# Modulation of layer 0 in a two-layer transformer kernel: weights as the stationary operand

## The chip, the cores and the metric

The kernel runs on one core of one Trainium2 chip. The metric is the device time of one execution in microseconds, taken as the median of a few runs. A profile of one execution goes with it. TensorE appears in the profile as two rows: PE for the streaming of the moving operand, PEld for the loading of the stationary operand.

## The reference, cut to what matters

Two transformer layers work on 1024 latent tokens and 256 context tokens of width 1024. Each layer starts from a modulation: a vector `silu(c)` for the latent tokens, and a second one, `silu(c_ctx)`, for the context tokens, are multiplied by the layer's `ada_w` (1024 x 6144). The first two sixths of the product are the shift and the scale of the first norm.

```
silu_c = jax.nn.silu(c);  silu_cc = jax.nn.silu(c_ctx)
mod_l = silu_c @ ada_w[i] + ada_b[i]      # and mod_c with silu_cc
sh1, sc1, g1, sh2, sc2, g2 = jnp.split(mod, 6)
a = rms_norm(h, norm_mix[i]) * (1.0 + sc1) + sh1
q, k, v = split(a @ w_qkv)                # then attention, output, FFN
```

The change concerns only shift and scale (`sh1`, `sc1`) of layer 0, which are needed before any projection of that layer can start: 1024 x 2048 weights, two input vectors.

## The kernel before, in words

Tensors lie by feature: 128 features on the partitions, eight blocks of features (`kc` or `m`, 0 to 7), tokens on the free axis. The tokens come in three blocks: 0 and 1 are the latent tokens (512 each), 2 is the context (256).

Everything of interest happens in `startup()`, the first 115 us. Its order is not left to a scheduler: each step is a generator, started at a planned time, and a heap of planned times decides in which order the instructions are written into the queues of the engines (TensorE, VectorE, ScalarE, GpSimd, and SyncE for all transfers). A planned time is thus only a rank. On the chip each engine takes its queue strictly in order and waits where an input is missing. The steps:

- `loads()` queues all transfers on SyncE: the eight modulation tiles `aw` (1 MB each, three buffers), the tokens `x` of block 0 between the first of them, raw weights of the first K, Q and V products, the tokens of blocks 1 and 2 (block 2 takes an `aw` buffer), two copies of the broadcast vectors to memory (`Cd`, for later modulations), more raw weights, and 40 small transfers for the position bias.
- `c_rows()` (L348 to L352) broadcasts the two silu vectors over all partitions: a diagonal on VectorE, a product with a matrix of ones on TensorE (four of 512 columns), a copy on ScalarE into `crow`.
- `stat(b)` (L363 to L382) gives the root mean square of a block: eight squares on ScalarE, six additions on VectorE and GpSimd, two products with ones on TensorE (L373), logarithm and exponential on ScalarE. Block 0 is then multiplied by the result on VectorE (L382).
- `modulation(m)` (L397 to L409), once for each block of features. The shift: two multiply-and-reduce passes of VectorE over the transposed weights and `crow` (L400), one for each vector. The scale: eight products on TensorE with the two vectors as the stationary operand and 128 columns of weights moving (L397), which gives two rows; ScalarE copies them out (L403), TensorE turns them into columns (L407). Three small VectorE instructions add the biases and form the gain (L404, L408, L409).
- `apply0(kc)` (L419 to L423) makes the normalised block 0 as a high part on ScalarE and a low part on GpSimd; `apply(b, kc)` (L431, L432, and `norm_lo` at L131 to L134) does the same for blocks 1 and 2, with VectorE in it.
- `first_qk(b)` (lines L770 to L772 in `dense_steps`) multiplies a block with the first K and Q weights, three products for each block of features because high and low parts are multiplied separately; `vals0` (L786 to L788 in `proj_v`) makes the V tiles, 128 tokens at a time. `first_qk(0)` takes block kc only after the modulation of block kc + 3 is written.

The queue order on TensorE from L373 on is, before: modulation 3 and 4, two kc of `first_qk(0)`, modulation 5, 6 and 7 with single kc between them, the other kc of block 0, four V tiles, block 1, two V tiles, block 2, four V tiles.

Of the kernel before, what the change touches and what calls it, by code (L numbers as in the profile page):

```python
# [10 lines left out]
F32 = mybir.dt.float32  # L11
F32R = mybir.dt.float32r
ALU = mybir.AluOpType
# [5 lines left out]
P = 128  # L19
D = 1024  # L20
KC = D // P
# [10 lines left out]

V_NMIX, V_NFFN, V_NFIN, V_B, V_QG, V_KG, V_C = 0, 16, 32, 40, 136, 137, 138
V_N = 154
CFG = dict(lag=3, tv=8.0, tm=5.0, t1=43.0, t2=58.0, p0=28, lo="GD", n=39, ra=2.3, rc=0.7, rq=1.1, rb=1.05, gap=263, r1=1.262, lh=300, tk='ADAG', tb=1000000000.0, tg=1, lp='GD')
PERIOD1 = 8172
ORDER1 = {
# [35 lines left out]
def _build(tc, nc, I, O, top):  # L73
    v, s, g, t = nc.vector, nc.scalar, nc.gpsimd, nc.tensor
# [17 lines left out]
    ident = const.tile([P, P], F32, name="ident")  # L92
# [6 lines left out]
    def vec(base, k):  # L99
        return vecs[:, base + k:base + k + 1]  # L100
# [166 lines left out]
    def startup():  # L267

        ET = mybir.EngineType
        with ExitStack() as ph:  # L270
# [29 lines left out]
            def loads():  # L300
                W = I["wqkv0"]
                for m in range(KC):
                    load_aw(m)
                    yield 2.9
                    if m < 2:
                        load_x(0, m)
                        yield 2.9
                    if m in (2, 4):
                        k = "k" if m == 2 else "q"
                        load_raw(k, W[8 if m == 2 else 0])  # L310
                        start(now + 3.5, split(k, wsp))
                        yield 1.5
                for i in range(2):
                    load_raw(f"v{i}", W[16:18, :, i * 512:i * 512 + 512])
                    start(now + CFG["tv"], split(f"v{i}", w0))
                    yield 1.5
                for i in range(2):
                    load_x(1, i)
                    yield 2.9
                xs.append(tmp.tile([P, KC, 256], F32, name="aw", bufs=3))  # L320
                load_x(2, 0, 1)
                yield 2.9
                for w in range(2):
                    dma(out=Cd[w], in_=crow[w][:])
                    yield 1.5
                for m in (1, 9):
                    load_raw(f"u{m}", W[m])
                    yield 1.5
                for _ in bias_steps():
                    yield 0.7  # L330
# [12 lines left out]
            def c_rows():  # L343
                for w in range(2):
                    for i in range(2):
                        ps = psm.tile([P, 512], F32, name="ps1")
                        dg = tmp.tile([P, 4, P], F32, name="nsq", bufs=2)
                        v.tensor_tensor(dg[:], ident[:].unsqueeze(1).broadcast_to([P, 4, P]),  # L348
                                        silc2[:, 4 * i:4 * i + 4, w:w + 1].broadcast_to([P, 4, P]), ALU.mult)
                        t.matmul(ps[:], lhsT=ones[:], rhs=dg[:].rearrange("p a n -> p (a n)"), start=True, stop=True)  # L350
                        yield 0.8
                        s.mul(crow[w][:, i * 512:i * 512 + 512], ps[:], float(D))  # L352
                        yield 0.3

            def stat(b):
                n = BLK[b][1]
                acc = []
                for kc in range(KC):
                    if b == 0 and kc == 4:
                        yield 3.6  # L360
                    sq = tmp.tile([P, n], F32, name="nsq", bufs=2) if kc > 1 else \
                        tmp.tile([P, n], F32, name=("nacc", "nacb")[kc], bufs=1)
                    s.activation(sq[:], xs[b][:, kc, :], AF.Square)  # L363
                    if kc > 1:
                        i = kc in (3, 6)
                        (v, g)[i].tensor_tensor(acc[i][:], acc[i][:], sq[:], ALU.add)
                    else:
                        acc.append(sq)
                    yield 0.55
                yield CFG["tm"] if b == 1 else 2.0  # L370
                ms = psp.tile([P, 512], F32, name="ms")
                for i in range(2):
                    t.matmul(ms[:, :n], lhsT=ones[:], rhs=acc[i][:], start=i == 0, stop=i == 1)  # L373
                yield 2.0
                rs[b] = tmp.tile([P, n], F32, name="nrs", bufs=1)
                s.activation(rs[b][:], ms[:, :n], AF.Ln, bias=eps[:])
                s.activation(rs[b][:], rs[b][:], AF.Exp, scale=-0.5)
                acts[b] = new_act(b)
                yield 0.9
                if b == 0:  # L380
                    for kc in range(KC):
                        v.tensor_tensor(xs[0][:, kc, :], xs[0][:, kc, :], rs[0][:], ALU.mult)  # L382
                        start(now + 0.9, apply0(kc))
                        yield 0.7
                    return
                for kc in range(KC):
                    start(now, apply(b, kc))
                    yield 1.1 if b == 1 else 0.7

            raw0 = tmp.tile([P, KC, 2], F32, name="raw0", bufs=1)  # L390
            ready = set()

            def modulation(m):

                rows = psp.tile([2, P], F32, name="rw", bufs=2)
                for kc in range(KC):
                    t.matmul(rows[:], lhsT=silc2[:, kc, :], rhs=aws[m][:, 1, kc * P:kc * P + P], start=kc == 0, stop=kc == KC - 1)  # L397
                for w in range(2):
                    junk = tmp.tile([P, D], F32, name="adaj", bufs=1)
                    v.tensor_tensor_reduce(junk[:], aws[m][:, 0], crow[w][:], 1.0, 0.0, ALU.mult, ALU.add, raw0[:, m, w:w + 1])  # L400
                yield 2.2
                rsb = tmp.tile([2, P], F32, name="rsb", bufs=2)
                s.copy(rsb[:], rows[:])  # L403
                v.tensor_scalar(modA[0][:, m, :], raw0[:, m, :], vec(V_B, m), 1.0, ALU.add, ALU.mult)  # L404
                yield 0.6
                cols = psp.tile([P, 2], F32, name="cl", bufs=1)
                t.transpose(cols[:], rsb[:], ident[:2, :2])  # L407
                v.tensor_scalar(modA[0][:, 8 + m, :], cols[:], vec(V_B, 8 + m), 1.0, ALU.add, ALU.add)  # L408
                v.tensor_scalar(G1[0][:, m, :], modA[0][:, 8 + m, :], vec(V_NMIX, m), 1.0, ALU.mult, ALU.mult)  # L409
                ready.add(m)  # L410

# [50 lines left out]
                start(now + 3.0, split("u9", wsp))  # L462
                yield from vals0((8, 9, 6, 7))

            for at, gen in [(0.0, loads()), (5.0, c_rows()), (10.0, stat(0)), (CFG["t1"], stat(1)), (CFG["t2"], stat(2)), (28.0, projections())] + \
                    [(max(9.5, a), modulation(m)) for m, a in enumerate((7.0, 13.0, 18.7, 23.0, 26.0, 30.4, 33.3, 36.2))]:
                start(at, gen)
            while todo:
                now, _, gen = heapq.heappop(todo)
# [1310 lines left out]
    with ExitStack() as ph:  # L1780
# [252 lines left out]
        n = CFG["n"]  # L2033
# [552 lines left out]
def layout(i):  # L2586
    perm = _perm()
    xT = _blocks(i["x"][0][perm])
    A = {}
    A["x0"], A["x1"] = xT[:, :, :512], xT[:, :, 512:]  # L2590
    A["x2"] = _blocks(i["ctx"][0])
    gq = i["gqa_q_gain"][0]
    gk = i["gqa_k_gain"][0]
    A["vecs"] = np.concatenate(
        [_col(i["norm_mix"]), _col(i["norm_ffn"]), _col(i["norm_final"]), _col(i["ada_b"]),
         np.concatenate([gq, gq])[:, None], np.concatenate([gk, gk])[:, None],
         _col(i["c"][0]), _col(i["c_ctx"])], axis=1)
    w = i["ada_w"][0][:, :2048].reshape(KC, P, 2, KC, P)
    A["ada0n"] = np.stack([w[:, :, 0].reshape(D, KC, P).transpose(1, 2, 0),
                           w[:, :, 1].transpose(2, 1, 0, 3).reshape(KC, P, D)], axis=2)  # L2600
    A["adaT0"] = i["ada_w"][0].T.reshape(48, P, D)
    A["adaT1"] = i["ada_w"][1].T.reshape(48, P, D)
    A["wqkv0"] = _units(i["na_w_qkv"][0])
    A["wo0"] = _units(i["na_w_o"][0])
    A["wqkv1"] = _units(i["gqa_w_qkv"][0])
    A["wo1"] = _units(i["gqa_w_o"][0])
    for l in range(2):
        A[f"fin{l}"] = _units(i["ffn_w_in"][l])
        A[f"fout{l}"] = i["ffn_w_out"][l].reshape(NJ, P, D)
    A["rpbp"] = np.pad(i["na_rpb"][0], ((0, 0), (8, 8), (0, 0)))  # L2610
    A["masks"] = _const_masks()
    A["rope"] = _const_rope()
    A["hones"] = np.kron(np.eye(2), np.full((HD, HD), 1.0 / HD)).astype(np.float32)
    return {k: np.ascontiguousarray(a, dtype=a.dtype) for k, a in A.items()}
# [23 lines left out]
```

## Time and profile before

| what | value |
|---|---|
| median of three runs | 3030.74 us (3030.30 to 3031.72) |
| profiled execution, its own time | 3030.41 us |
| its span, first to last instruction | 3028.6 us |
| TensorE clock granted, mean | 0.992 of full |
| `startup()` on TensorE | 0 to about 115 us |

An execution takes some 1.8 us more than the span that the profile shows. Busy times are unions of overlapping instructions. A line of the timeline or of the chain has the start in microseconds, the duration, the engine and the line of code; in brackets stands the idle time before it and what ended it. A line of a table by stretches has the sum of busy time for each engine with the number of instructions, then the granted TensorE clock, the share of the DMA engines and GB/s. TensorE runs at full or at half clock; the table shows which was granted.

### The profile page before, as it was taken

What the parts mean: (1) busy time and instruction counts of PE and PEld (TensorE: products, weight loads), DVE (VectorE), ACT (ScalarE), POOL (GpSimd) and SP (SyncE); (2) the same over time, 40 slices, a digit from 0 to 9 for tenths busy, and PEclk for the clock granted to TensorE, in tenths of its full rate; (3) what the DMA queues carried; (4) which work ended last, traced back from release to release, by engine and by line L of the source; (5) the groups of instructions that cost most, each with busy time, mean ns of one, the idle gap of its engine ahead of it and who ended that gap; (6) DMA issues with size and microseconds to landing.
All of it is one profiled execution on the core that took longest, in us unless ns stands there. A gap on an engine that the chain in (4) does not pass through costs nothing.

```text
span 3028.6 us, 50110 instructions
## 1 busy us (share of the span) xinstructions
PE 2917.2 (96%) x16460; PEld 2503.2 (83%) x16460; DVE 2304.4 (76%) x4659; ACT 1621.8 (54%) x3739; POOL 1245.6 (41%) x1109
## 2 busy tenths in 40 slices
PE   7999998899999999999999899999999999999998
PEld 4788997788788888888889788888888878888886
DVE  7588778776698785557777588899887887776776
ACT  4345545766652222224456488898887632333444
POOL 4246556766234451121121256666643344223112
PEclk9999999999999999999999999999999999999999
DMA  7777777787535562239656523333323443224962
GB/s 265 218 228 242 225 223 226 226 233 207 201 129 195 195 225 85 96 127 330 213 190 215 167 86 93 100 102 105 111 73 122 139 139 118 105 105 147 325 216 108
DMA packets 307170, 519.03 MB, mean 171 GB/s; under 512 B 46432, under 2 KB 112096, under 8 KB 305120
## 3 DMA queue, kind: packets, MB, share of 16 engines
q1 hardware_dynamic: 306912, 515.84, 52.6%
q8 instruction: 131, 2.15, 0.3%
q14 instruction: 127, 1.04, 0.1%
HBM read 389.61 MB, written 120.18 MB: 168 GB/s over the span
## 4 chain that ended last, share of the span: by engine, by line
PE 77%; DVE 9%; DMA 5%; ACT 3%; POOL 3%; issue 2%; SPq 1%; DVEq 0%; POOLq 0%; ACTq 0%
PE pf L1461 9%; PE pf L1462 9%; PE pf L1463 9%; PE T L867 5%; PE o L497 5%; PE pf L1711 5%; PE pf L1710 5%; PE pf L1709 5%; PE ps L770 3%; PE ps L771 3%; PE ps L772 3%; DMA K<-Kd 2%; PE S L2246 2%; PE S L2247 2%; DVE pT L880 1%
## 5 line engine op out<-in xcount | busy, mean ns | idle before, releaser
L860 POOL TENSOR_SCALAR Pt<-Pt,rc 128x1280 f32<-128x1280 f32 (+3 forms) x288 | 299.4, 1040 | 389.0 <-ACT pT L875 143.8
L875 ACT CAST pT<-T 128x256 fp32r<-128x256 f32 (+2 forms) x672 | 305.0, 477 | 124.7 <-PE T L867 120.1
L880 DVE TENSOR_TENSOR pT<-T,pT 128x256 fp32r<-128x256 f32 (+2 forms) x672 | 341.7, 534 | 31.2 <-ACT pT L875 30.8
L867 PE MATMUL T<-ident,Pt 128*128 128x128 f32 x1952 | 302.5, 274 | 23.8 <-POOL Pt L860 22.9
L867 PEld LDWEIGHTS T<-ident,Pt 128*128 128x128 f32 x1952 | 235.2, 140 | 79.6 <-POOL Pt L860 35.4
L497 PE MATMUL o<-pT,Vt 128*128 128x256 f32 x1952 | 295.6, 290 | 2.3 <-DVE pT L880 2.2
L770 PE MATMUL ps<-ah,wh 128*128 128x512 f32 (+1 forms) x688 | 261.3, 380 | 5.5 <-ACT ah L432 2.6
L497 PEld LDWEIGHTS o<-pT,Vt 128*128 128x128 f32 x1952 | 254.3, 189 | 9.5 <-DVE pT L880 5.7
L771 PE MATMUL ps<-al,wh 128*128 128x512 f32 (+1 forms) x688 | 251.5, 366 | 5.3 <-POOL al L132 3.6
L849 ACT ACTIVATE Pt<-S,rc 128x512 f32<-128x512 f32 (+2 forms) x384 | 247.4, 654 | 9.6 <-DVE rc L841 6.5
L772 PE MATMUL ps<-ah,wl 128*128 128x512 f32 (+1 forms) x688 | 250.9, 365 | 1.4 <-DVE wl L338 1.4
L2238 DVE TENSOR_REDUCE nm<-S 128x1 f32<-128x512 f32 x256 | 169.6, 682 | 35.8 <-PE S L2247 34.1
L952 POOL TENSOR_TENSOR c<-c,c 128x512 f32<-128x512 f32 (+1 forms) x63 | 92.6, 1472 | 248.7 <-DVE c L955 89.5
L955 DVE TENSOR_TENSOR c<-c,c 128x512 fp32r<-128x512 f32 (+1 forms) x166 | 131.3, 804 | 48.5 <-ACT c L1437 34.6
L849 ACT ACTIVATE Pt<-X,rc 128x256 f32<-128x256 f32 x256 | 125.2, 489 | 65.3 <-DVE rc L841 58.6
L1437 ACT CAST wh<-c 128x512 fp32r<-128x512 f32 x112 | 68.9, 618 | 166.9 <-PE pf L1462 66.8
L895 POOL TENSOR_TENSOR r<-ob 128x256 f32<-128x256 f32 x144 | 123.7, 859 | 65.4 <-ACT ob L889 58.7
L772 PEld LDWEIGHTS ps<-ah,wl 128*128 128x128 f32 x688 | 131.1, 191 | 23.3 <-DVE wl L338 2.1
L771 PEld LDWEIGHTS ps<-al,wh 128*128 128x128 f32 x688 | 132.0, 192 | 18.5 <-POOL al L132 5.2
L770 PEld LDWEIGHTS ps<-ah,wh 128*128 128x128 f32 x688 | 131.5, 191 | 18.6 <-ACT ah L432 2.8
L1461 PE MATMUL pf<-c,wh 128*128 128x512 f32 x376 | 146.5, 390 | 0.0
L1462 PE MATMUL pf<-c,wh 128*128 128x512 f32 x376 | 146.5, 390 | 0.0
(599 smaller groups left out, 9155.3 us busy)
## 6 DMA issues: line engine op xcount, KB each, us to landing
c<-in_fout SPq DMA_DIRECT2D x119, 256.0 KB, 4.0
wr<-in_wqkv SPq DMA_DIRECT2D x53, 512.0 KB, 4.2
wr<-in_adaT SPq DMA_DIRECT2D x96, 256.0 KB, 3.2
c<-in_fin SPq DMA_DIRECT2D x68, 256.0 KB, 2.9
adaw<-in_adaT SPq DMA_DIRECT2D x64, 256.0 KB, 4.0
wr<-in_wo SPq DMA_DIRECT2D x32, 512.0 KB, 4.5
wr<-in_fin SPq DMA_DIRECT2D x58, 256.0 KB, 2.7
K<-Kd SPq DMA_DIRECT2D x64, 224.0 KB, 4.6
```

Of the source, the lines that this page charges most:

```text
L497: t.matmul(o_ap, lhsT=u.V[:, kb, :], rhs=u.pT[:, i, :], start=i == 0, stop=i == len(u.blocks) - 1)
L770: t.matmul(ps, lhsT=hi[:, c], rhs=ah[:, kc, :n], start=kc == 0, stop=False)
L771: t.matmul(ps, lhsT=hi[:, c], rhs=al[:, kc, :n], start=False, stop=False)
L772: t.matmul(ps, lhsT=lo[:, c], rhs=ah[:, kc, :n], start=False, stop=kc == KC - 1)
L849: s.activation(u.Pt[:, off:off + u.wid[c]], u.S[c], AF.Exp, bias=u.min, scale=u.sign, accum_out=u.rc[:, 3 + c:4 + c])
L860: g.tensor_scalar(Pt, Pt, u.rc[:, 2:3], 1.0, ALU.mult, ALU.mult)
L867: t.transpose(T[:, i * P:(i + 1) * P], u.Pt[:, (i0 + i) * P:(i0 + i + 1) * P], ident[:])
L875: s.copy(u.pT[:, i0:i0 + n, :P], u.T[c])
L880: v.tensor_tensor(u.pT[:, i0:i0 + n, P:], u.T[c], u.pT[:, i0:i0 + n, :P].bitcast(F32), ALU.subtract)
L1461: t.matmul(ps[:], lhsT=r32(hi[:, c]), rhs=bh, start=k == 0, stop=False)
L1462: t.matmul(ps[:], lhsT=r32(hi[:, c]), rhs=bl, start=False, stop=False)
L1463: t.matmul(ps[:], lhsT=r32(lo[:, c]), rhs=bh, start=False, stop=k == 3)
```

## The change: what it does

The tile `aw[m]` now holds both halves, shift and scale, in the same layout (features of the input on the partitions). For each half, eight products take 128 x 128 weights as the stationary operand and the two vectors as two moving columns, accumulated into columns of PSUM: `[128, 4]`, shift and scale for both vectors. The result is by feature, so the reduction on VectorE, the copy on ScalarE and the transposition are gone; three small VectorE instructions stay. `c_rows()` is still there, since `Cd` feeds later modulations, but nothing in `startup()` waits for `crow` any more except `Cd`; it is started at a planned time of 17.5 instead of 5.0. The planned starts of the modulations, of `stat(1)` and `stat(2)` and of the splitting of the V weights are new too.

```
-CFG = dict(lag=3, tv=8.0, tm=5.0, t1=43.0, t2=58.0, ...)
+CFG = dict(lag=3, tv=4.0, tm=5.0, t1=39.0, t2=50.0, ...)
...
 def modulation(m):
-    rows = psp.tile([2, P], F32, name="rw", bufs=2)
-    for kc in range(KC):
-        t.matmul(rows[:], lhsT=silc2[:, kc, :], rhs=aws[m][:, 1, kc * P:kc * P + P], start=kc == 0, stop=kc == KC - 1)
-    for w in range(2):
-        junk = tmp.tile([P, D], F32, name="adaj", bufs=1)
-        v.tensor_tensor_reduce(junk[:], aws[m][:, 0], crow[w][:], 1.0, 0.0, ALU.mult, ALU.add, raw0[:, m, w:w + 1])
-    yield 2.2
-    rsb = tmp.tile([2, P], F32, name="rsb", bufs=2)
-    s.copy(rsb[:], rows[:])
-    v.tensor_scalar(modA[0][:, m, :], raw0[:, m, :], vec(V_B, m), 1.0, ALU.add, ALU.mult)
-    yield 0.6
-    cols = psp.tile([P, 2], F32, name="cl", bufs=1)
-    t.transpose(cols[:], rsb[:], ident[:2, :2])
-    v.tensor_scalar(modA[0][:, 8 + m, :], cols[:], vec(V_B, 8 + m), 1.0, ALU.add, ALU.add)
+    cols = psp.tile([P, 4], F32, name="cl", bufs=2)
+    for i in range(2):
+        for kc in range(KC):
+            t.matmul(cols[:, 2 * i:2 * i + 2], lhsT=aws[m][:, i, kc * P:kc * P + P], rhs=silc2[:, kc, :],
+                     start=kc == 0, stop=kc == KC - 1)
+    yield 3.0
+    v.tensor_scalar(modA[0][:, m, :], cols[:, 0:2], vec(V_B, m), 1.0, ALU.add, ALU.mult)
+    v.tensor_scalar(modA[0][:, 8 + m, :], cols[:, 2:4], vec(V_B, 8 + m), 1.0, ALU.add, ALU.add)
     v.tensor_scalar(G1[0][:, m, :], modA[0][:, 8 + m, :], vec(V_NMIX, m), 1.0, ALU.mult, ALU.mult)
...
-(5.0, c_rows()) ... modulation(m) at max(9.5, a) for a in (7.0, 13.0, 18.7, 23.0, 26.0, 30.4, 33.3, 36.2)
+(17.5, c_rows()) ... modulation(m) at 5.5, 11.5, 17.0, 21.0, 24.5, 29.0, 32.0, 35.0
...
-A["ada0n"] = np.stack([w[:, :, 0].reshape(D, KC, P).transpose(1, 2, 0),
-                       w[:, :, 1].transpose(2, 1, 0, 3).reshape(KC, P, D)], axis=2)
+A["ada0n"] = np.stack([w[:, :, i].transpose(2, 1, 0, 3).reshape(KC, P, D) for i in range(2)], axis=2)
```

The queue order after, as the planned times give it. On TensorE: modulation 0, 1, 2, two products of `c_rows`, a third, the two of `stat(0)`, the fourth of `c_rows`, modulation 3, 4, 5, two kc of `first_qk(0)`, modulation 6, one kc, modulation 7, five kc, then V tiles and blocks 1 and 2 in the order of before. On ScalarE the logarithm of block 0 stands behind the four copies of `c_rows`; the logarithm of block 1 moves from behind the third V tile to behind the second; the squares of block 2 move from among the high parts of block 1 to, for the larger part, ahead of them. On SyncE the first `Cd` transfer moves from ahead of the K and Q results of block 0 to behind them.

More of the change, by code (lines that the diff above doesn't have):

```diff
@@ L34 @@
 V_N = 154
-CFG = dict(lag=3, tv=8.0, tm=5.0, t1=43.0, t2=58.0, p0=28, lo="GD", n=39, ra=2.3, rc=0.7, rq=1.1, rb=1.05, gap=263, r1=1.262, lh=300, tk='ADAG', tb=1000000000.0, tg=1, lp='GD')
+CFG = dict(lag=3, tv=4.0, tm=5.0, t1=39.0, t2=50.0, p0=28, lo="GD", n=39, ra=2.3, rc=0.7, rq=1.1, rb=1.05, gap=263, r1=1.262, lh=300, tk='ADAG', tb=1000000000.0, tg=1, lp='GD')
 PERIOD1 = 8172
@@ L388, in stat @@
                     yield 1.1 if b == 1 else 0.7
-            raw0 = tmp.tile([P, KC, 2], F32, name="raw0", bufs=1)
             ready = set()
             def modulation(m):
-                rows = psp.tile([2, P], F32, name="rw", bufs=2)
-                for kc in range(KC):
-                    t.matmul(rows[:], lhsT=silc2[:, kc, :], rhs=aws[m][:, 1, kc * P:kc * P + P], start=kc == 0, stop=kc == KC - 1)
-                for w in range(2):
-                    junk = tmp.tile([P, D], F32, name="adaj", bufs=1)
-                    v.tensor_tensor_reduce(junk[:], aws[m][:, 0], crow[w][:], 1.0, 0.0, ALU.mult, ALU.add, raw0[:, m, w:w + 1])
-                yield 2.2
-                rsb = tmp.tile([2, P], F32, name="rsb", bufs=2)
-                s.copy(rsb[:], rows[:])
-                v.tensor_scalar(modA[0][:, m, :], raw0[:, m, :], vec(V_B, m), 1.0, ALU.add, ALU.mult)
-                yield 0.6
-                cols = psp.tile([P, 2], F32, name="cl", bufs=1)
-                t.transpose(cols[:], rsb[:], ident[:2, :2])
-                v.tensor_scalar(modA[0][:, 8 + m, :], cols[:], vec(V_B, 8 + m), 1.0, ALU.add, ALU.add)
+                cols = psp.tile([P, 4], F32, name="cl", bufs=2)
[6 more added lines that the diff above has]
+                v.tensor_scalar(modA[0][:, 8 + m, :], cols[:, 2:4], vec(V_B, 8 + m), 1.0, ALU.add, ALU.add)
                 v.tensor_scalar(G1[0][:, m, :], modA[0][:, 8 + m, :], vec(V_NMIX, m), 1.0, ALU.mult, ALU.mult)
@@ L463, in projections @@
                 yield from vals0((8, 9, 6, 7))
-            for at, gen in [(0.0, loads()), (5.0, c_rows()), (10.0, stat(0)), (CFG["t1"], stat(1)), (CFG["t2"], stat(2)), (28.0, projections())] + \
-                    [(max(9.5, a), modulation(m)) for m, a in enumerate((7.0, 13.0, 18.7, 23.0, 26.0, 30.4, 33.3, 36.2))]:
+            for at, gen in [(0.0, loads()), (17.5, c_rows()), (10.0, stat(0)), (CFG["t1"], stat(1)), (CFG["t2"], stat(2)), (28.0, projections())] + \
+                    [(a, modulation(m)) for m, a in enumerate((5.5, 11.5, 17.0, 21.0, 24.5, 29.0, 32.0, 35.0))]:
                 start(at, gen)
```

## The prediction

> **What bounds the kernel now.** I read the page first.
>
> ```profile
> span 3028.6 us, 50110 instructions
> PE 2917.2 (96%) x16460; PEld 2503.2 (83%) x16460; DVE 2304.4 (76%) x4659; ACT 1621.8 (54%) x3739; POOL 1245.6 (41%) x1109
> ```
>
> Over the whole span TensorE (PE) is the bound. A change in the first 60 us is judged by those 60 us, so the next view is busy time by stretches (PE, PEld, DVE, ACT, POOL, then the granted clock).
>
> ```profile
> 20.00:30.00 10.00, 4.25 (x23) 2.35 (x24) 9.90 (x18) 3.90 (x8) 2.89 (x3) 0.95 0.67 235
> 30.00:40.00 10.00, 8.26 (x30) 4.58 (x30) 9.93 (x13) 2.40 (x4) 10.00 (x6) 0.50 0.60 224
> 40.00:50.00 10.00, 10.00 (x59) 6.58 (x58) 9.79 (x15) 1.92 (x4) 9.19 (x6) 0.86 1.01 395
> ```
>
> Here VectorE is full (9.9 of 10) and TensorE is not: it runs the second stretch at half clock. The chain of waits shows what VectorE does, and the groups of the first 60 us how much of it.
>
> ```profile
> 50.40 0.23 DVE G L409
> 50.63 1.12 DVE adaj L400
> 51.80 1.67 DVE adaj L400
> 53.51 1.15 DVE modA L404
> ...
> 54.82 0.24 DVE G L409
> 55.08 0.82 ACT ah L419
> ...
> L400 DVE CUSTOM_DVE_ANT_0 adaj<-aw,crow 128x1024 f32<-128x1024 f32 x16 | 21.8, 1361 | 1.3 <-ACT crow L352 1.1
> L397 PE MATMUL rw<-aw,silc 128*2 128x128 f32 x128 | 18.6, 308 | 0.9 <-DMA aw<-in_ada0n 0.9
> L423 POOL TENSOR_TENSOR al<-nx,ah 128x512 fp32r<-128x512 f32 x8 | 14.6, 1831 | 0.4
> L421 POOL TENSOR_SCALAR nx<-x,G,modA 128x512 f32<-128x512 f32 x8 | 13.7, 1711 | 8.8 <-DVE x L382 7.1 <-DVE G L409 1.5
> ```
>
> One modulation follows the other at 54.82 - 50.40 = 4.4 us, all of it VectorE, and the last gain (54.82) releases the last high part. The first block's products end just behind it, and the rest of the start-up hangs on them:
>
> ```profile
> 58.41 0.39 PE L772 MATMUL ps<-ah,wl 128*128 128x512 f32 x1
> 58.64 0.28 PE L786 MATMUL ps<-wh,ah 128*128 128x256 f32 x1
> 58.75 0.28 PE L787 MATMUL ps<-wh,al 128*128 128x256 f32 x1
> ...
> 92.37 0.39 PE L772 MATMUL ps<-ah,wl 128*128 128x512 f32 x1
> ```
>
> Call 58.6 T, the end of block 0's K and Q products. A product of 512 columns takes 0.23 from start to start (58.41 to 58.64), one of 256 columns 0.115. Block 1's end 34 us after T (92.6).
>
> **The change, part by part: removed.** VectorE loses the sixteen reductions, 21.8 us; ScalarE eight small copies, TensorE eight transpositions and the 128 passes of L397. With VectorE free, the next thing late is TensorE's own queue, so its sum decides.
>
> **Added: 256 weight loads.** One 32-bit product shows as two passes (eight products of a modulation are 16 of the 128 passes). The new modulation has 16 products, so 32 passes, each a load of 128 x 128 weights and only two moving columns. No row of before has such a pass; the price of a load is bounded by these (minimum / median / maximum of the durations in ns, and four TensorE rows):
>
> ```profile
> L397 PEld LDWEIGHTS rw<-aw,silc x128: 81/85/127, 9.7 to 49.2; 128*2 128x2 f32 x128
> L373 PEld LDWEIGHTS ms<-nacb,ones x6: 188/190/190, 21.1 to 86.1; 128*128 128x128 f32 x6
> L350 PEld LDWEIGHTS ps<-nsq,ones x8: 191/310/337, 3.7 to 8.8; 128*128 128x128 f32 x8
> ...
> 3.72 6.09 PE L350 MATMUL ps<-nsq,ones 128*128 128x512 f32 x8 [3.72 <-DVE nsq L348]
> 9.75 1.91 PE L397 MATMUL rw<-aw,silc 128*2 128x128 f32 x16
> 21.57 1.02 PE L373 MATMUL ms<-nacb,ones 128*128 128x512 f32 x2
> 29.91 3.57 PE L397 MATMUL rw<-aw,silc 128*2 128x128 f32 x16
> ```
>
> At full clock a load of 128 columns lasts 190 ns and one of 2 columns 85 ns: 126 columns cost 105 ns. At half clock it is 337 against 127: 210 ns. So the columns go in at 0.107 us for 128 of them, 0.213 at half clock, and the other 80 to 120 ns is latency, which the next load can hide. From below the pass is 0.107 us, because the array takes no more columns; from above it is 0.19, if a load cannot start under the previous pass. The L770 to L772 passes do overlap (a load for each 0.115), so I take 0.11: a modulation is 32 x 0.11 = 3.5 us of TensorE, at half clock 32 x 0.213 = 6.8. Eight are 28 us, where L397 took 18.6 in the shadow of VectorE.
>
> The Trainium skill, "TensorE: Matmul & The Clock Gate", section "LDWEIGHTS (loading the stationary operand)", prices a load by its columns over 1.2 GHz, 107 ns whatever the clock. At full clock the rows agree; at half clock the 337 against 190 ns contradict it. By that rule a modulation would cost 3.4 us at either clock, and the first rival below would cost nothing.
>
> **The sum to T.** TensorE's queue starts with modulation 0 when its tile has landed. Bytes by slices of 2.5 us, the transfers behind, and two GpSimd pieces used further down:
>
> ```profile
> GB/s 64 321 416 433 423 429 419 413 408 123 334 75 374 3 134 384 366 429 413 374 197 10 0 0 205 321 290 321 168 113 121 24 24 25 19 19 222 169 327 261
> ...
> 23.03 12.42 SPq L81 DMA_DIRECT2D aw<-in_ada0n  x3
> 38.32 0.98 SPq L81 DMA_DIRECT2D x<-in_x  x2
> ...
> 55.15 0.78 POOL L421 TENSOR_SCALAR nx<-x,G,modA 128x512 f32<-128x512 f32 x1 [0.51 <-DVE G L409]
> 56.05 1.28 POOL L423 TENSOR_TENSOR al<-nx,ah 128x512 fp32r<-128x512 f32 x1
> ```
>
> The first 5 us move 0.96 MB, so the first tile (1.05 MB) is there at about 5.4. Then: 8 x 3.5 = 28; the broadcast products, which used to run in a wait, 4 x 0.93 = 3.7 (two passes each, a pass of 512 columns about 0.465: twice 0.23); `stat(0)`'s two products, 1.9; block 0, 48 x 0.23 = 11. That is 44.6. The first 3.4 us or so run at half clock, as L350 did, which costs half of it, 1.7. Modulation 2 waits for its tile (third MB of weights, fifth in all, 15.1 by the same bytes, TensorE free at 14): 1. The products of `c_rows` wait for VectorE's diagonals: 0.5. T = 5.4 + 44.6 + 3.2 = 53.2; taking 0.115 a pass instead of 0.11 adds 1.3. I use T = 54, 4.6 earlier.
>
> What hides the rest. Transfers: the three `aw` loads that held SyncE for 12.42 us waited for buffers; TensorE now frees them at 24 (`stat` and `c_rows` done) + 3.5 each, so the last tile comes at about 36, needed at 42, and the `x` loads are issued before 38.32. Block 0's logarithm now waits for `c_rows` on TensorE and ScalarE: first high part at about 27, covered since block 0's products start at 35. Behind it lies GpSimd: eight pieces at 1.71 + 1.83 = 3.5 us would end at 27 + 28 = 55. Those durations belong to a full VectorE; beside an idle one (55.15, 56.05) they were 0.78 and 1.28, giving 27 + 17 = 44. VectorE is now about half busy, so about 49.5, under TensorE's last kc at 52. If that cover goes, T is 57.
>
> **Behind T: the new ranks of `stat(1)` and `stat(2)`.** Between T and 92.6 TensorE has 4 tiles x 24 x 0.115 = 11, 48 x 0.23 = 11 and the `stat` products, about 3: 25 of 34 us. Nine are waiting, on these:
>
> ```profile
> 74.31 0.49 PE L770 MATMUL ps<-ah,wh 128*128 128x512 f32 x1 [2.56 <-ACT ah L432]
> 81.04 1.68 DVE L366 TENSOR_TENSOR nacc<-nacc,nsq 128x256 f32<-128x256 f32 x2 [1.10 <-ACT nsq L363]
> ...
> ACT vt L792 <- DMA Vd<-vt: 5.5, 2, 5.0
> ```
>
> ScalarE waits 5 us for a V tile's buffer with block 1's logarithm behind it; and VectorE waits for squares of block 2 (81.04) while block 1's pieces queue behind them. Both orders are undone. The wait for the V tile itself stays, and the moved `Cd` transfer adds 0.5 MB in front of it, 1.2 us at 420 GB/s. Bounds are 0 and 9; I take 6, as VectorE's conflict goes fully and the other half. From 92.6 on TensorE hardly waits, and the page's 96% says that a shift passes on; 1 us off for transfers that do not move with it. Gain 4.6 + 6 - 1 = 9.6: 3030.4 - 9.6 = 3020.8, and with the median 0.3 above the profiled execution, 3021. A difference under 0.2% (6 us) cannot be told from none.
>
> **The rivals.** First, TensorE at half clock. These are stretches as long as the clock's steps (the half-clock period starts at 29.3 and ends at 42.95):
>
> ```profile
> 15.64:19.06 3.42, 1.91 (x16) 1.28 (x16) 2.90 (x7) 1.48 (x4) 0.33 (x1) 1.00 1.03 426
> 25.88:29.30 3.42, 0.00 (x0) 0.00 (x0) 3.39 (x7) 0.78 (x2) 1.63 (x2) 0.96 0.51 168
> 29.30:32.71 3.41, 2.99 (x15) 1.85 (x16) 3.37 (x6) 2.51 (x5) 3.41 (x3) 0.50 0.75 303
> 39.54:42.95 3.41, 3.41 (x15) 2.01 (x14) 3.38 (x5) 0.96 (x2) 3.28 (x3) 0.54 1.02 362
> ```
>
> A stretch without work drops the clock, one with 1.91 of 3.41 keeps it, and only a full one raises it (2.99 did not). In all of them busy means columns streaming. The new modulations stream two columns a pass and load the rest of the time. If loads do not count, they look idle: three modulations at 6.8 us end at 26, `c_rows` and `stat(0)` raise the clock within some 8 us (34), modulation 3 takes 5.2, 4 and 5 take 6.8 each (53), two kc at half clock 5, modulation 6 6.8, a kc 2.6, modulation 7 6.8 (74), five kc 7 and about 2 for raising the clock: T = 83, 24.4 later. With the gain behind T, 3030.4 + 24.4 - 6 = 3049. Against it: a 100% busy array is nowhere seen at half clock for long. It decides from the fourth modulation at half clock on (4 x 3.3 - 1.7 against the 9.6 gained). Chance 0.34. The same page of the Trainium skill ("Part 4: PE-mode transpose") says that transpositions do not count as busy in the way of products; no run here shows it for loads.
>
> Second, loads hold the clock but don't raise it. Then modulations 0 to 2 run at half clock, 3 x 3.3 = 10 instead of 1.7 us lost: T = 62.5, and the gain behind T leaves 3029, no change that can be measured. 0.11.
>
> Third, T as forecast, but the new ranks bring nothing, since the wait for V buffers or GpSimd takes the place of what is removed: 3030.4 - 4.6 = 3026, within 0.2%. 0.09.
>
> **The numbers.** The forecast has 0.46. Its own range, T 53 to 57 and 2.5 to 9 behind it, is 3016 to 3027. Faster by over 0.2% is nearly all of it and a little of the second rival, 0.45; same is the second, the third and the rest of the forecast, 0.20; slower is the first, 0.35. The range reaches from 3016 over the second and third cases into the first one's 3049: 3016 to 3051 leaves out less than 2 in 10.
>
> **What would show it.** No L400 row; VectorE under 6 of 10 between 20 and 50. The new modulation row: 32 passes in 3.5 us at clock 1.0 (right), near 6.8 at 0.5 (first rival), half-clock only before `c_rows` (second). TensorE without gaps from 24 to T, T near 54. The first product of block 1 within 15 us of T and its last within 28 (third rival: 34). The forecast is wrong if T is above 58.6, or if the pass costs more than 0.13 us at full clock.

## The result and the profile after

The changed kernel takes 3054.62 us (median of four runs, 3052.65 to 3055.93), the kernel before on the same chip 3030.52 (3029.24 to 3031.72, four runs). The ratio is 1.0077, 95% interval 1.0061 to 1.0093: 24 us slower, where 9.6 us faster was forecast. The profiled execution took 3052.65 us with a span of 3050.7, so it stands 22.2 us behind the profiled execution of before (3030.41).

First the stretches of the changed kernel, in the columns of the table shown of before (sum, then PE, PEld, VectorE, ScalarE, GpSimd, granted clock, DMA share, GB/s), and then three stretches as long as the clock's steps.

```profile
30.00:40.00 10.00, 10.00 (x52) 7.26 (x50) 4.30 (x12) 5.58 (x9) 2.43 (x3) 0.92 0.23 81
40.00:50.00 10.00, 10.00 (x49) 10.00 (x49) 7.31 (x9) 2.44 (x3) 10.00 (x7) 0.50 0.62 222
60.00:70.00 10.00, 10.00 (x43) 9.42 (x43) 2.12 (x4) 2.70 (x3) 2.05 (x2) 0.50 0.01 3
```

```profile
31.52:34.93 3.41, 3.41 (x11) 1.57 (x10) 0.41 (x1) 0.95 (x3) 0.00 (x0) 1.00 0.04 17
34.93:38.34 3.41, 3.41 (x33) 3.41 (x32) 1.29 (x2) 2.62 (x5) 0.77 (x1) 1.00 0.00 0
38.34:41.75 3.41, 3.41 (x18) 3.41 (x18) 3.35 (x6) 2.47 (x4) 3.41 (x4) 0.50 0.66 226
```

VectorE is no longer full (9.93 and 9.79 before, 4.30 and 7.31 now), as intended. TensorE has no gap, and from 40 to 50 and 60 to 70 it is at half clock. The second table shows how it got there: the products of 512 columns have raised the clock at 31.52, one stretch of 3.41 us holds nothing but passes of the new modulation, and behind that stretch the same passes go at half speed (18 in 3.41). The clock's records begin with the step at 31.52; the half clock ahead of it is read from the passes themselves, which take as long as those behind 38.34.

The timeline of TensorE up to T shows the price of it, and the groups of the first 90 us its sum (busy time, mean ns of one).

```profile
6.97 20.61 PE L398 MATMUL cl<-silc,aw 128*128 128x2 f32 x96 [6.97 <-DMA aw<-in_ada0n]
27.44 4.84 PE L350 MATMUL ps<-nsq,ones 128*128 128x512 f32 x6
32.98 1.02 PE L373 MATMUL ms<-nacb,ones 128*128 128x512 f32 x2
33.84 1.02 PE L350 MATMUL ps<-nsq,ones 128*128 128x512 f32 x2
34.69 17.15 PE L398 MATMUL cl<-silc,aw 128*128 128x2 f32 x96
56.26 4.48 PE L398 MATMUL cl<-silc,aw 128*128 128x2 f32 x32
63.31 6.82 PE L398 MATMUL cl<-silc,aw 128*128 128x2 f32 x32
...
79.68 0.28 PE L780 MATMUL ps<-wh,ah 128*128 128x256 f32 x1
```

The row at 34.69 in a window that ends at 38.15, where the clock is still full:

```profile
34.69 3.63 PE L398 MATMUL cl<-silc,aw 128*128 128x2 f32 x32
```

```profile
L398 PEld LDWEIGHTS cl<-silc,aw 128*128 128x128 f32 x256 | 49.4, 301 | 7.7 <-issue 7.4
L398 PE MATMUL cl<-silc,aw 128*128 128x2 f32 x256 | 49.1, 329 | 7.0 <-DMA aw<-in_ada0n 7.0
```

The first 96 passes take 20.61 us, 0.215 each: half clock from the first to the last, with never a gap. The last 32 take 6.82, again 0.213. The first 32 of those at 34.69, behind the wide products, run at full clock (3.63, 0.113 each), and the 32 at 56.26, which follow some of block 0's products, mostly. T, the end of block 0's K and Q products, is 79.68, where it was 58.64.

Two places behind T matter further down. The first is the start of block 1 on TensorE and on VectorE, the second what SyncE does around block 1's results.

```profile
92.89 0.46 PE L764 MATMUL ps<-ah,wh 128*128 128x512 f32 x1
97.09 0.80 PE L765 MATMUL ps<-al,wh 128*128 128x512 f32 x1 [3.74 <-DVE al L134]
...
113.42 0.40 PE L766 MATMUL ps<-ah,wl 128*128 128x512 f32 x1
```

```profile
95.95 0.43 DVE L366 TENSOR_TENSOR nacc<-nacc,nsq 128x256 f32<-128x256 f32 x1 [1.09 <-ACT nsq L363]
96.29 0.75 DVE L134 SCALAR_TENSOR_TENSOR al<-nx,modA,ah 128x512 fp32r<-128x512 f32 x1
```

Block 1 starts 13.2 after T (15.7 before) and ends 34.0 after T, to the tenth what it was before. Its first low part stands on VectorE behind an addition of block 2, which waits 1.09 us for a square.

To follow the shift through the program, the start of the same TensorE instruction was compared in both traces, counted from the end of the program. The table has, for each kernel of this study, how much later (+) than in the kernel before this instruction starts; the time at the head of a column is that of the kernel before.

| kernel | T | 92.4 (block 1 ends) | 118 | 138 | 300 | end |
|---|---|---|---|---|---|---|
| changed kernel | +21.0 | +21.1 | +22.7 | +30.3 | +26.2 | +22.2 |
| n32 | +13.7 | +13.7 | +15.4 | +23.4 | +24.0 | +21.4 |
| n64 | +4.4 | +4.4 | +6.1 | +13.3 | +13.0 | +12.6 |
| n128 | -2.5 | -2.5 | -0.8 | +6.5 | +6.7 | +10.4 |
| n128_crow5 | -5.1 | -5.0 | -3.4 | +3.1 | +3.6 | +2.2 |
| ranks_only | +1.6 | +0.9 | +8.3 | +8.3 | +2.1 | +1.2 |
| n128_oldranks | -2.7 | -1.7 | -1.2 | -1.2 | -1.3 | -6.4 |
| n128_crow5_oldranks | -7.0 | -5.5 | -5.0 | -5.0 | -4.8 | -4.5 |
| after_oldranks | +20.3 | +22.8 | +23.3 | +23.3 | +24.6 | +21.8 |
| crow5_bias55 | -5.6 | -5.6 | -3.9 | -3.7 | -5.0 | +1.6 |
| crow5_t1_bias55 | -6.3 | -7.7 | -4.9 | -4.9 | -5.5 | -2.9 |
| n128_crow5_oldranks_again | -5.6 | -4.4 | -3.9 | -3.9 | -4.5 | -7.9 |

Each row is one profiled execution. The columns up to 300 follow the order of the work; the last row is n128_crow5_oldranks profiled a second time, and the two differ by 1.4 at T and 1.1 at 138, so a difference of that size says nothing here. Between 300 and the end every kernel gains or loses some us for reasons of its own (below), so for the end the medians decide.

The changed kernel loses 21 us by T and another 7.6 between 118 and 138. The second loss was in no part of the prediction.

### The profile page after: what moved, and what is told of

The parts are those of the page before. It is cut to its first block, busy times and chain, and to the rows that moved or that the text cites. A ratio compares the mean times of both kernels' runs of the same rounds, so it can differ in the third digit from the quotient of the medians.

```text
span 3050.7 us, 50300 instructions
## 1 busy us (share of the span) xinstructions
PE 2948.8 (97%) x16580; PEld 2543.5 (83%) x16580; DVE 2274.3 (75%) x4627; ACT 1620.2 (53%) x3731; POOL 1240.6 (41%) x1109
## 4 chain that ended last, share of the span: by engine, by line
PE 74%; DVE 9%; DMA 5%; ACT 3%; POOL 2%; issue 2%; SPq 1%; DVEq 0%; ACTq 0%; POOLq 0%
PE pf L1455 9%; PE pf L1456 9%; PE pf L1457 9%; PE T L861 5%; PE o L491 5%; PE pf L1705 5%; PE pf L1703 5%; PE pf L1704 5%; PE ps L764 3%; PE ps L766 3%; PE ps L765 3%; PE S L2240 2%; PE S L2241 2%; DMA K<-Kd 2%; DVE pT L874 1%
## 5 line engine op out<-in xcount | busy, mean ns | idle before, releaser
L861 PE MATMUL T<-ident,Pt 128*128 128x128 f32 x1952 | 302.0, 274 | 21.1 <-POOL Pt L854 20.5
```

What stands on the lines that cost most here:

```text
L861: t.transpose(T[:, i * P:(i + 1) * P], u.Pt[:, (i0 + i) * P:(i0 + i + 1) * P], ident[:])
```

## The experiments

**The clock.** Theory: the clock follows the columns that stream, and a weight load is no activity. Rival: loads of 128 columns are slow by themselves in this place, or TensorE's queue is simply longer than reckoned. The edit leaves every load as it is and widens the moving operand by repeating the two vectors, to 32, 64 or 128 columns; only the first two columns of each result are used.

```
-cols = psp.tile([P, 4], F32, name="cl", bufs=2)
+cols = psp.tile([P, 2, 128], F32, name="cl", bufs=2)
...
-t.matmul(cols[:, 2 * i:2 * i + 2], lhsT=aws[m][:, i, kc * P:kc * P + P], rhs=silc2[:, kc, :],
+t.matmul(cols[:, i], lhsT=aws[m][:, i, kc * P:kc * P + P], rhs=silc2[:, kc, :].unsqueeze(1).broadcast_to([P, 64, 2]),
```

> The changed kernel, with the moving operand of the modulation products repeated to 128 columns (64 copies of the two vectors), so that each pass streams 128 columns while the next weights load. Theory of the clock (TensorE's clock follows the streamed columns only, and loads look idle): passes at 0.11 us from about 14 us on, no half-clock stretch between the start and block 0's end, eight modulations in about 31 us instead of 49, block 0's products end at about 57 to 59 instead of 79.7, time 3028 to 3034. Rival (the loads are slow by themselves or TensorE's queue is simply too long, the clock is a by-product): more columns can only add work, passes of 0.11 or more at the same half clock, block 0 ends at 80 or later, time 3054 or more.

> The same with 64 columns: a pass at full clock streams 64 columns in 0.053 of 0.11 us, about half of the time. Theory of the clock, with the limits that the first kernel's trace shows (a stretch with 1.9 of 3.4 us kept the clock, 3.0 did not raise it): the clock is not raised by modulations 0 to 2 (0.213 a pass), it is raised by the broadcast products and then held, modulations 3 to 7 at 0.11 a pass, block 0 ends at about 64 to 66, one time about 3037 to 3041. Rival: as the changed kernel, block 0 at 80, 3054.

> The same with 32 columns: 0.027 of 0.11 us streaming, a quarter. Theory of the clock: not enough to hold it (stretches under about a third lost it in the first kernel's trace), so block 0 ends at about 79 to 80 and the time is 3053 to 3056, as with two columns. If one column or two are not what decides but any widening helps, it would lie between 3035 and 3050.

The modulations on TensorE's timeline, for 128, then 64, then 32 columns:

```profile
6.86 13.77 PE L398 MATMUL cl<-silc,aw 128*128 128x128 f32 x96 [6.86 <-DMA aw<-in_ada0n]
27.28 10.90 PE L398 MATMUL cl<-silc,aw 128*128 128x128 f32 x96
40.77 3.74 PE L398 MATMUL cl<-silc,aw 128*128 128x128 f32 x32
```

```profile
6.29 20.71 PE L398 MATMUL cl<-silc,aw 128*128 128x64 f32 x96 [6.29 <-DMA aw<-in_ada0n]
34.20 10.83 PE L398 MATMUL cl<-silc,aw 128*128 128x64 f32 x96
```

```profile
6.33 20.66 PE L398 MATMUL cl<-silc,aw 128*128 128x32 f32 x96 [6.33 <-DMA aw<-in_ada0n]
33.83 17.41 PE L398 MATMUL cl<-silc,aw 128*128 128x32 f32 x96
55.40 3.65 PE L398 MATMUL cl<-silc,aw 128*128 128x32 f32 x32
...
60.36 3.65 PE L398 MATMUL cl<-silc,aw 128*128 128x32 f32 x32
```

The same 256 loads, in the same order, with more columns behind each. With 128 columns the clock rises within the first 96 passes (13.77 us) and stays up: the next 96 take 10.90, 0.1135 each, which is the price with 2 columns at full clock (0.113). With 64 it doesn't rise on its own (20.71), but once the products of 512 columns have raised it, it stays (10.83). With 32 it neither rises nor stays (20.66 and 17.41). T is 79.7, 72.4, 63.0 and 56.2 for 2, 32, 64 and 128 columns, and the times are 3054.6, 3051.85 and 3043.03 (one run each for 32 and 64) and 3037.69 (ten runs). The rival falls: 64 times the columns to stream makes the passes faster. With 32 columns T comes 7 us earlier than with 2, which was not expected (79 to 80). In both, block 0's products raise the clock ahead of modulation 6; it then stays up for 10.24 us with 32 columns (54.31 to 64.55), so that modulations 6 and 7 take 3.65 each, and for 3.41 us with 2 (55.41 to 58.82), where they take 4.48 and 6.82. What these 32 columns add to the products between them, and what the place of the steps does, was not separated.

The clock alone doesn't explain the time, though. With 128 columns T lies 2.5 us ahead of before, and the kernel is still slower: 1.0011 (1.0002 to 1.002), 3037.69 where 3028 to 3034 was expected.

**The rows of `c`.** A fourth kernel puts `c_rows()` back to its planned time of before, on top of the 128 columns.

```
-(17.5, c_rows())
+(5.0, c_rows())
```

> 128 columns, and the broadcast products planned at 5.0 as in the first kernel, ahead of modulation 0. Theory of the clock: they run in the wait for the first tile (TensorE idle to 7.0), raise the clock by about 9 us, and no longer stand between modulation 2 and 3; modulation 0 starts at about 9.8 instead of 7.0, all passes at 0.11; block 0 ends at about 53 to 55, time 3024 to 3028. Rival: half clock through the modulations whatever comes first, block 0 at 75 or later, 3050.

T is 53.56, 5.1 us ahead of before: the first of its products now runs at 3.85 to 5.92, before the first tile is there, the waits for VectorE's diagonals (0.78 and 0.35 in n128) are gone, and the clock is up from 10.97 in place of 12.36. The time is 3038.19, ratio 1.0018 (1.0006 to 1.003): nothing of the 5 us arrives (3024 to 3028 was expected). The table above says where they go: -3.4 at 118, +3.1 at 138. n32, n64, n128 and the changed kernel lose about as much on the same stretch, whatever their T.

**The planner's numbers.** What these kernels have in common there, and the kernel before doesn't, is the order in SyncE's queue. In n128 it is this (start, duration, count of a group of transfers):

```profile
74.88 10.01 SPq L81 DMA_DIRECT2D E<-in_rpbp  x15
95.92 0.34 SPq L81 DMA_DIRECT2D Kd<-qh  x1
...
98.01 1.24 SPq L81 DMA_DIRECT2D E<-in_rpbp  x2
101.75 1.18 SPq L81 DMA_DIRECT2D Bd<-E  x2
...
124.28 5.69 SPq L81 DMA_DIRECT2D K<-Kd  x8
```

and in the kernel before, in the same view:

```profile
88.25 1.84 SPq L81 DMA_DIRECT2D Bd<-E  x3
93.01 0.34 SPq L81 DMA_DIRECT2D Kd<-qh  x1
...
117.82 5.06 SPq L81 DMA_DIRECT2D K<-Kd  x8
```

In n128 the store of block 1's K result stands ahead of the last two E transfers and all the sixteen Bd transfers of the position bias; in the kernel before all E and three Bd go first. SyncE issues nothing from 84.9 to 95.92, because it waits for that result; everything that could have gone meanwhile goes behind it. Its waits between 80 and 100 us say the same (released by, us in all, times, longest):

```profile
SPq L81 <- ACT qh L806: 10.9, 1, 10.9
```

The wait is so long because the result itself is late. On ScalarE it stands behind block 2's high parts, and is made at 95.31, 5 us after block 1's last product; in the kernel before it is made at 92.41, right with that product.

```profile
94.90 0.51 ACT L426 ACTIVATE ah<-nx,modA 128x256 fp32r<-128x256 f32 x1 [0.91 <-DVE nx L425]
95.31 1.06 ACT L806 ACTIVATE qh<-ps 128x512 fp32r<-128x512 f32 x2
```

The theory was that this costs the 7 us: the kernel before with nothing but the new numbers must show it, and the kernels with the new modulation and the old numbers must not.

```
-tv=8.0, tm=5.0, t1=43.0, t2=58.0     (before)
+tv=4.0, tm=5.0, t1=39.0, t2=50.0     (ranks_only)
```

> The kernel before with nothing but the change's three planner numbers (tv 4, t1 39, t2 50 in place of 8, 43, 58). The end of block 0's K/Q products, T, stays at 58.6. Theory 'ranks': block 1's Kd and Qd stores now stand on SyncE ahead of the last two E transfers and of all Bd transfers and hold them up until block 1's K/Q results are there, some 92 to 96; the first Bd starts near 98 to 102 in place of 88.25, the loads of K at the start of attention some 6 us later than 117.82, and TensorE at the point that the kernel before reaches at 138 some 6 to 7 us later; 3034 to 3038, ratio 1.001 to 1.003. Rival 'the ranks cost nothing' (the 7 us come from the earlier T or the wider products, not from the order): TensorE at 138 within 1.5 us of before, ratio 0.9995 to 1.0005.

> The 128-column version with the planner numbers of before. T near 56.2 as with the new ranks. Theory 'ranks': the first Bd starts by 90 and the 2.5 us ahead are kept through 138 (TensorE there 1 to 4 us earlier than before); 3027 to 3029 where before stands at 3030.5, ratio 0.9985 to 0.9997. Rival 'the ranks cost nothing': TensorE at 138 some 6 us later than before, as with the new ranks, ratio 1.001 to 1.002.

> The 128-column version, the rows of c planned at 5.0 as before, and the planner numbers of before. T near 53.5. Theory 'ranks': the 5 us ahead are kept through 138 (3 to 6 us earlier than before), less what attention's own limits give back; 3025 to 3028, ratio 0.998 to 0.9993. Rival 'the ranks cost nothing': 3 us later than before at 138, ratio 1.000 to 1.002. A third: attention takes its own pace from its transfers, so that what is gained by 138 is gone by 300; ratio 0.9997 to 1.0005.

> The changed kernel (two moving columns) with the planner numbers of before. T stays near 79.7 (21 later than before). Theory 'ranks': at 138 TensorE is 20 to 23 us later than before, not 30; 3046 to 3053, ratio 1.005 to 1.0075. Rival 'the ranks cost nothing': 28 to 31 us later at 138, ratio 1.007 to 1.009.

With the new numbers alone the kernel before is at +8.3 at 138, and slower: 3037.3 us, ratio 1.0021 (1.001 to 1.0031). It loses this between 92 and 118, where TensorE waits 4.1 us for a V tile, and its one trace has 6.2 us of it back by 300; the median still stands 7.7 us behind. With the old numbers the loss is gone from all three kernels: -1.2 at 138 in place of +6.5, -5.0 in place of +3.1, +23.3 in place of +30.3. The times follow for 128 columns: 3027.67, ratio 0.999 (0.9978 to 1.0002), and with the rows of `c` at 5.0 3026.22, ratio 0.9991 (0.9981 to 1.0). They don't for the changed kernel: 3053.9, ratio 1.0075 (1.0056 to 1.0094), against 1.0077 with the new numbers. There the 7 us at 138 are 1.7 by 300 (+26.2 against +24.6), and four runs each can't tell the rest.

The waits from 112 to 145 us show how SyncE's order reaches TensorE, first in n128, then in n128_oldranks (engine, line, what it waited for: us in all, times, longest).

```profile
ACT vt L786 <- DMA Vd<-vt: 9.6, 2, 9.4
...
PE ps L764 <- DVE ql L808: 4.0, 2, 3.2
```

```profile
ACT qh L806 <- DMA Qd<-qh: 7.9, 1, 7.9
...
ACT vt L786 <- PE ps L782: 2.5, 1, 2.5
```

In n128 ScalarE waits 9.4 us for a buffer of a V tile, whose store stands on SyncE behind the delayed Bd transfers; in its queue behind that wait stand the splits of the next weights and the next K and Q results, and TensorE waits 3.2 us for one of those (4.0 in all) and loses the clock (125.00 to 131.83 at half, some 3.4 us of time): together the 7.3 us between 118 and 138. With the old numbers the wait for a V store isn't there; ScalarE still waits for a Q store (7.9), but TensorE goes from 118 to 138 without losing anything (-1.2 at both).

**Is it SyncE's order, or the order of the other engines?** The new numbers also interleave block 2's squares with block 1's pieces on VectorE, ScalarE and GpSimd. Two more runs separate this, and a third is a repeat. The first keeps all the new numbers and only plans the bias transfers more closely, which puts E and the first four Bd ahead of block 1's K store; the second has that and, of the new numbers, only `t1`. The third is the fastest version so far on the chip of those two.

```
 for _ in bias_steps():
-    yield 0.7
+    yield 0.55
```

> The 128-column version with the rows of c at 5.0 and all three new planner numbers; beside them only the pace at which the E and Bd transfers are planned is 0.55 in place of 0.7, which puts E and the first Bd transfers ahead of block 1's Kd and Qd on SyncE again, while the new order on VectorE, ScalarE and GpSimd stays. Theory 'SyncE's order is the price of the new numbers': T near 52 to 54; the first Bd starts before block 1's Kd; TensorE at the point that the kernel before reaches at 138 is 3 to 6 us earlier than before, as with the old numbers; ratio 0.998 to 0.9995. Rival 'the other engines' new order is the price': 2 to 4 us later at 138, as with the pace of 0.7; ratio 1.000 to 1.002.

> The same, but of the planner numbers only t1 (39) is new: block 1's squares come sooner and block 2's stay behind block 1's first steps. Theory A 'the gain behind T that was forecast is real, and the interleaved squares of block 2 took it': block 1's last product ends 29 to 32 after T, against 34 in the kernel before; 6 to 10 us earlier than before at 138. Theory B 'block 1 is held by something else (V's products, its own chain)': 33.5 to 36 after T, as with the old numbers, 3 to 6 us earlier at 138; ratio 0.998 to 0.9995.

> The version that came out fastest, once more on the same chip as the two others of this call, to compare with them. T 52 to 54, 5 us earlier than before at 138; 3025 to 3028 where before stands at 3030, ratio 0.998 to 0.9997. If the earlier 0.9991 was chance: 0.9995 to 1.001.

SyncE in crow5_bias55:

```profile
71.79 10.67 SPq L81 DMA_DIRECT2D E<-in_rpbp  x16
84.83 2.50 SPq L81 DMA_DIRECT2D Bd<-E  x4
92.83 0.34 SPq L81 DMA_DIRECT2D Kd<-qh  x1
...
114.53 5.06 SPq L81 DMA_DIRECT2D K<-Kd  x8
```

The first Bd starts at 84.83 in place of 101.75 (n128), the loads of K at 114.53 in place of 124.28, and at 138 the kernel is 3.7 us ahead of before, with all three new numbers in place. The K result is as late as in n128 (its store goes 5.8 us after block 1's last product in both), so ScalarE's order lengthens the wait, but only SyncE's order makes it cost time; the rival falls. The times are 3024.11 for crow5_bias55, ratio 0.9973 (0.9962 to 0.9984); 3026.55 for crow5_t1_bias55, 0.9982 (0.9968 to 0.9995); 3024.39 for the repeat, 0.9976 (0.9965 to 0.9987), twelve runs each. These three are 0.2 to 0.3% faster than the kernel before, with intervals below 1, and can't be told from one another. The repeat had 0.9991 (0.9981 to 1.0) on another chip, so the size is known to some 0.15%.

The second of them was also to show whether the 6 us that were forecast behind T are there once block 2's squares are out of the way. Block 1's last product ends at 84.91, 32.6 after T, between the two theories (29 to 32, 33.5 to 36). But two `stat` products of block 2 stand behind it here and ahead of it in the other kernels; with them it is 33.3. With the old numbers it is 34.9 to 36.5 in the kernels with the new modulation, with all the new ones 34.0. So the new numbers are worth 1 to 2.5 us behind T, not 6. Without the interleaved squares TensorE waits 0.9 us at most for a low part of VectorE's instead of 3.7, but 1.7 for V's weights and 2.7 instead of 1.3 for GpSimd, so that 0.7 us are left of it.

## Why the prediction was wrong, point by point

**The passes of the new modulation: right in both sizes, wrong in which applies.** The prediction had 0.11 us a pass at full clock and 0.213 at half. Measured are 0.113 (3.63 over 32) and 0.213 (6.82 over 32). It then took the full clock for all but the first 3.4 us: "a modulation is 32 x 0.11 = 3.5 us", "eight are 28 us". This is the step that failed. The eight took 49.1 us, since the clock was at half up to 31.52 and from 38.34 to 75.89, but for 55.41 to 58.82.

The reason for the choice was that in before no busy array stays at half clock for long. But the busy stretches of before hold products that stream 128 columns or more, with the loads beside them. The trace of before could not show whether loads are activity, and the prediction gave the forecast the greater chance on the strength of that silence. Its first rival said what the runs then showed: three modulations at half clock, products that raise it, one modulation that still profits, then half clock again. It put T at 83 and the time at 3049, with 0.34.

**The sum to T: 53.2, measured 79.7.** The difference of 26.5 has three parts. The modulations are 21.1 longer than 28, of which 1.7 were allowed for: 19.4. Block 0's products and those of `stat(0)` and `c_rows` take 79.68 - 6.97 - 49.1 = 23.6, where 3.7 + 1.9 + 11 and 1.5 of waits were reckoned: 5.5 more, the same half clock on other instructions. The first tile landed at 6.97 instead of 5.4: 1.6. The rival's 83 was 3.3 too late, mostly in modulation 6, which it had at 6.8 and which took 4.48 behind block 0's products. The price of a load in the Trainium skill ("TensorE: Matmul & The Clock Gate", section "LDWEIGHTS (loading the stationary operand)"), 107 ns whatever the clock, is near the 0.113 a pass and is contradicted by the 0.213. In the same page ("Why this matters for your kernels") some 4 us of continuous work are said to bring the full clock; 20.61 us of passes without a gap did not, so work there has to be read as columns streaming.

Where the clock does rise, the rest of the sum holds. In n128 it is up from 12.36 and T is 56.2, where the sum gives 53.2: the tile is 1.5 late, 5.5 us of passes run at half clock instead of 3.4, and the waits for diagonals are 1.1 instead of 0.5. With the rows of `c` at 5.0, T is 51.6 to 53.6.

**What hides the rest: right.** VectorE fell to 4.3 and 7.3 of 10 (under 6 was expected), no tile, no logarithm and no GpSimd piece held TensorE, which has no gap from 6.97 to T. There TensorE was later than all of it. In n128, where it was not, GpSimd is busy 9.85 and 9.28 of 10 from 30 to 50 and TensorE still waits for none of it.

**Behind T: 6 us forecast, about 0 measured.** The step read two waits in before (5 us of ScalarE on a V buffer, VectorE on squares of block 2) and took them to be undone by the new order. One came back in another place: block 1's first low part waits behind an addition of block 2, 3.74 us of TensorE at 97.09. The prediction's third rival, that the new numbers bring nothing there and block 1's last product stays 34 after T, held to the tenth in the changed kernel, though the old numbers with the new modulation would have given 36.5.

**Not in the prediction: SyncE.** The text counted one moved transfer (`Cd`, 1 us). It did not carry the earlier rank of `stat(1)` on to what hangs on it: the K and Q stores of block 1, which moved in SyncE's queue past the first Bd and the last E, so that all the Bd, which need nothing of block 1, now stand behind them (eighteen transfers in n128, thirteen in the kernel before). This is 7 to 8 us at 138 in every kernel with the new numbers and the old pace, and 0.2 to 0.4% of the time with 128 columns: 1.0011 against 0.999, and 1.0018 against 0.9991 and 0.9976, each against the kernel before on its own chip.

**The size.** Rival one with its own terms right (T 21.0 later in place of 24.4, and nothing behind T in place of 6) gives 3030.4 + 21 = 3051.4, to which comes what is left of SyncE's loss; measured 3052.65 in the profiled execution. The range's upper end, 3051, was drawn from the rival's point value and had no room for a rival whose gain fails.

**Open.** By 300 the changed kernel gives back 4.1 of what it had lost at 138, and ranks_only 6.2; n128 gives back nothing. In the traces TensorE waits 5.5 and 4.9 us for GpSimd's pieces of attention on that stretch in the first two, 8.3 in the kernel before and 9.9 in n128, and ranks_only has no step to half clock there where the kernel before has two (6.83 us). Why those waits are shorter was not tried.

## What to carry to other kernels

Weights as the stationary operand with a few moving columns keep TensorE's queue full and its clock at half: either stream columns enough (64 held the clock here, 128 raised it), which cost nothing here (0.1135 us a pass with 128 columns, 0.113 with 2, both at full clock), or leave wide products between. When a computation moves in a queue written by hand, its stores move with it, and a store that waits holds up every transfer behind it that waits for nothing.

## What the runs showed of the hardware beyond that

How much must stream can be estimated from the rows. The modulation is in full 32-bit type, like the products of L350 and L373, and of those two passes of 512 columns take 0.86 us at full clock (32.98 to 33.84), 0.43 each, not the 0.23 of block 0's products. So 64 columns are 0.054 of a pass of 0.113, about half, and held the clock, while 32 columns, about a quarter, did not in a stretch of nothing else; at half clock 64 columns are again half and did not raise it, and 128, the whole pass, did. So it takes less to hold the clock than to raise it. The kernel before agrees: 1.91 of 3.41 us kept the clock, and 2.99 did not raise it (the stretches in the prediction lie 0.24 us behind the steps, which came at 29.06 and 42.71; moved there they hold 1.91 and 2.75, and the readings stay).

Late in the program the clock drops for 3.41 us or two or three times that, at places that change from one execution to the next. In the profiled execution of crow5_bias55 the records have 34 us at half clock between 210 and 1800 us, against 17 in the kernel before, which makes up to 8.5 us of time; it went from -5.0 at 300 to +1.6 at the end, and took 3031.99 where the median of its twelve runs is 3024.11. The clock isn't all of it: n128_oldranks has as much half clock there as the kernel before (17 us) and gains 5.1 between 300 and the end. Executions of the kernel before on that chip range from 3022.46 to 3042.67. A change of 5 us in the first 100 is seen at once in one trace at 138 or 300, and needs ten runs or more in the time.
